# Two small MLPs of an attention branch, side by side on the columns of the array

## The chip, the cores and the metric

The kernel runs on one core of one Trainium2 chip. The metric is the device time of one execution in microseconds (us), a median over runs; less is better. A core has TensorE (PE; its weight loads are listed apart, as PEld), VectorE (DVE), ScalarE (ACT), GpSimd (POOL) and SyncE (SP), which here only issues DMAs.

## The reference

A two-layer decoder trunk on 512 tokens of width 1024. Each layer makes one input projection and hands parts of it to three token mixers: a gating MLP (its two inputs are za0 and za1 below), a retention, and a sparse attention. The last one has a compressed branch: keys and values of overlapping blocks of 32 tokens pass through a small MLP, one for the keys and one for the values.

```python
def compress(kv, pos_emb, w1, w2):
    Bn, S, G, d = kv.shape
    nc = (S - CMP_BLOCK) // CMP_STRIDE + 1          # 31 blocks
    idx = (jnp.arange(nc) * CMP_STRIDE)[:, None] + jnp.arange(CMP_BLOCK)[None, :]
    blocks = kv[:, idx] + pos_emb[None, None, :, None, :]
    flat = jnp.moveaxis(blocks, 3, 2).reshape(Bn, nc, G, CMP_BLOCK * d)
    return jax.nn.gelu(flat @ w1) @ w2              # (., 2048) @ (2048, 64), then @ (64, 64)
...
k_cmp = compress(k_c.reshape(Bn, S, G, d), pos_k, w1_k, w2_k)
v_cmp = compress(v_c.reshape(Bn, S, G, d), pos_v, w1_v, w2_v)
...
sc = jnp.einsum('bqgrd,bkgd->bgrqk', qb, k_cmp)
p_cmp = masked_softmax(sc, cmp_end[None, :] <= t[:, None])
o_cmp = jnp.einsum('bgrqk,bkgd->bqgrd', p_cmp.astype(dt), v_cmp)
```

## The kernel before

Each layer runs through the same stages on the core. Weights come from HBM through a ring of three raw buffers, issued on SP in a fixed order of jobs; ACT makes a rounded part of each (L125), DVE or, for some, POOL the difference (L127), and every large product is three PE passes on those parts (L535 to L537 for projections with tokens as rows, 128x256; L445 to L447 for those with features as rows). Where a projection is named a step, it is twelve such products: `tm_all` yields after each step, and four steps make half of za0 or za1.

The input projection first makes the raw keys and values of the compressed branch and the queries. `compress_in` (L497, DVE) adds the position embedding and writes F, one tile for the keys and one for the values: its free dimension is ordered head half, group, block, position, with eight positions innermost. `compress_load` fetches the weights: `w1` as sixteen blocks of 128x64 for each MLP, `w2` as a small tile.

Then za0 is projected (`tm_all`, ending in a GELU on ACT, L732). Then the compressed branch stands alone on PE: `compress_mm` multiplies the sixteen blocks of w1 with 62 columns of F, which lie eight values apart (L506), for the keys and then for the values, each in float32 into partitions 0 to 63 of its own PSUM tile. ACT applies GELU (L741 to hk, L744 to hid, a tile named t in the trace), PE multiplies with w2 (L747 for the keys, L749 twice for the values, named cw), ACT copies the keys out (L752, kc), DVE the values with a mask (L756, vcs), and `cmp_scores` multiplies kc with the queries on four 32-column strips of the array (L688), DVE adding a mask (L691, cs). Only then za1 is projected, its GELU giving Vv (L732).

Behind it come the projection of values and gates (L535 to L537 with 280 columns), the normalization of Vv on DVE (`norm64`, L464 to L475, with a power on POOL, L471), the softmax of the compressed scores (`cmp_softmax`, L699 to L715) between two key projections, and the transposes of its result (L724). In layer 1 `last_gains` also scales the residual xa by the gain and bias rows of the previous norm, two DVE passes a token tile (L1134, L1135 inside `gains`): tiles 0 and 1 behind the compressed branch, 2 and 3 behind za1.

The order on an engine is the program's, as a scheduler with a simulated timeline arranges it when the program is built; an engine then runs its list in order. PSUM has eight banks, given out in turn by `ps()`. For comparison, `retention` has products of the same shapes: L901 (128x64 weights, 64 columns, outputs alternating between partitions 0 and 64) and L892 (64 rows, alternating between the halves of the rows).

Of the kernel before, what the change touches and what calls it, by code (L numbers as in the profile page):

```python
# [22 lines left out]
L = 2  # L23
HD = 64
# [59 lines left out]
class Weights:  # L84
# [45 lines left out]
    def next(self, key, ahead=AHEAD, loads=3):  # L130
        i = self.i
        assert self.jobs[i][0] == key, (self.jobs[i][0], key)
        self.i += 1
        self.split(i)
        r = self.parts.pop(i)
        self.parts[i] = None
        raw = r.__class__ is not tuple
        for j in range(i + 1, i + 1 + ahead):
            if j < len(self.jobs) and self.jobs[j][1] != "raw":
                for j2 in range(i + 1, j):  # L140
                    self.load(j2)
# [7 lines left out]
def tile_trunk(ctx, tc, I, tab, out, layers=L):  # L149
    nc = tc.nc  # L150
    V, A, G, T = nc.vector, nc.scalar, nc.gpsimd, nc.tensor
# [3 lines left out]
    pool = ctx.enter_context(tc.tile_pool(name="sb", bufs=1))  # L155
    psum = ctx.enter_context(tc.tile_pool(name="ps", bufs=8, space=bass.MemoryType.PSUM))

    def ps():
        return psum.tile([P, 512], F32, tag="ps", name="ps")

    def t2(dt=F32):
        return pool.tile([P, 512], dt, tag="t2", name="t2", bufs=4)

    def m4(name):
        return pool.tile([P, 1024], F32, tag="m4", name=name, bufs=5)

    def big(name, dt=F32):
        return pool.tile([P, 13 * P], dt, tag="big", name=name, bufs=4)
# [13 lines left out]
    def load(dst, src):  # L182

        tc.keep_in_program_order(nc.sync.dma_start(dst, src))
# [47 lines left out]
    for l in range(layers):  # L232
# [16 lines left out]
        for n in range(32):  # L249
            if n % 8 in (0, 2):  # L250
                nm, c0 = (("rq", C_QB), ("rk", C_KB), ("rv", C_VB), ("rg", C_GB))[n // 8]
                h = n % 8 // 2
                job_cols((nm, l, h), l, [(c0, 256)], 4 * h, 4 * h + 4)
            if n in ADA_AT and aj:
                j = aj.pop(0)
# [25 lines left out]
    def tabv(name):  # L281
        a, b = TAB[name]
        return tb[:, a:b]
# [102 lines left out]
    def run(g):  # L386
        for _ in g:
            pass
# [89 lines left out]
    def compress_load(l):  # L478
        w1 = []
        for nm in ("c_w1_k", "c_w1_v"):  # L480
            w = big("w1")[:, :1024].rearrange("p (m e) -> p m e", m=16)
            load(w, I[nm][l].rearrange("(m p) e -> p m e", p=P))
            w1.append(w)
        w2 = pool.tile([P, 2, 256], F32, tag="al", name="cw2", bufs=1)[:64, :, :P]
        load(w2[:, 0, 0:64], I["c_w2_k"][l])
        load(w2[:, 0, 64:128], I["c_w2_k"][l])
        load(w2[:, 1, 0:64], I["c_w2_v"][l])
        return w1, w2

    def compress_in(pk, pos):  # L490
# [8 lines left out]
                                    op=OP.add)  # L499
        return F  # L500

    def compress_mm(F, w1):
        pc = ps()
        for m in range(16):
            h = m // 8
            T.matmul(pc[:64, :62], w1[:, m, :], F[:, h, :, h:h + 31, m % 8], start=(m == 0), stop=(m == 15))  # L506
        return pc

    for l in range(layers):
# [20 lines left out]
        def tm(wt, o, t, n, k0, k1, first, last):  # L530

            wh, wl = [w[:, :(k1 - k0) * n].rearrange("p (k n) -> p k n", n=n) for w in wt]
            for k in range(k0, k1):
                a, b = hx(hh, k, t, t + 1), hx(hl, k, t, t + 1)
                T.matmul(o, a, wh[:, k - k0, :], start=(first and k == 0), stop=False)  # L535
                T.matmul(o, a, wl[:, k - k0, :], start=False, stop=False)  # L536
                T.matmul(o, b, wh[:, k - k0, :], start=False, stop=(last and k == KD - 1))  # L537

        def tm_all(key, done):

            wts = []
            for tp in range(2):
                bank = ps()
                for h in range(2):
                    if not tp:
                        wts.append(ws.next(key + (h,)))
                    for s_ in range(2):
                        tm(wts[h], bank[:, s_ * 256:(s_ + 1) * 256], 2 * tp + s_, 256, 4 * h, 4 * h + 4,
                           s_ == 0, s_ == 1)
                        if h and s_:  # L550
                            done(tp, bank)
                        yield
# [13 lines left out]
        cmp_ps = []  # L566
        if l:
# [3 lines left out]
            for j in range(4):  # L571
                if j == 2:
                    last_h()
                banks.append(ps())
                wts.append(fm(keys[j], banks[j], 0))
            w1, w2 = compress_load(l)
            for j in range(6):
                if j < 4:
# [8 lines left out]
        else:  # L587
# [83 lines left out]
            for t in range(NT):  # L671
                G.tensor_scalar(X[t], X[t], ALPHA, None, op0=OP.mult)
            par = params(l)
            w1, w2 = compress_load(l)
            for j in range(2):
                cmp_ps.append(compress_in(banks[4 + j], par["pos"][j]))
# [7 lines left out]
        def cmp_scores(kc):  # L684
            for g in range(2):
                pc = ps()
                for r in range(4):
                    T.matmul(pc[32 * r:32 * r + 32, :], kc[:, g * 32:(g + 1) * 32], Q[g][:, r, :].bitcast(F32),  # L688
                             start=True, stop=True, tile_position=(0, 32 * r))
                CS.append(pool.tile([P, 512], F32, tag="yc", name="cs", bufs=2))  # L690
                V.tensor_tensor(CS[g], pc, mcmpb, op=OP.add)  # L691
# [36 lines left out]


        U, Vv = m4("U"), m4("Vv")  # L730
        for j, (nm, dst) in enumerate((("za0", U), ("za1", Vv))):
            run(tm_all((nm, l), lambda tp, pz, dst=dst: A.activation(  # L732
                dst[:, tp * 512:(tp + 1) * 512], pz, AF.Gelu_apprx_tanh)))
            if j == 0:

                hid = t2()[:64, :256].rearrange("p (g r n) -> p g r n", g=2, r=4)
                hk = pool.tile([64, 2, 32], F32, tag="hk", name="hk", bufs=1)
                G.memset(hid, 0.0)
                G.memset(hk, 0.0)
                pc = compress_mm(cmp_ps[0], w1[0])  # L740
                A.activation(hk[:, :, 0:31], pc[:64, :62].rearrange("p (g n) -> p g n", g=2), AF.Gelu_apprx_tanh)  # L741
                pc = compress_mm(cmp_ps[1], w1[1])
                for g in range(2):
                    A.activation(hid[:, g, :, 0:31],  # L744
                                 pc[:64, None, g * 31:(g + 1) * 31].to_broadcast([64, 4, 31]), AF.Gelu_apprx_tanh)
                pc = ps()
                T.matmul(pc[:, 0:64], w2[:, 0, :], hk.rearrange("p g n -> p (g n)"), start=True, stop=True)  # L747
                for g in range(2):
                    T.matmul(pc[:, 64 + 64 * g:128 + 64 * g], hid[:, g].rearrange("p r n -> p (r n)"),  # L749
                             w2[:, 1, 0:64], start=True, stop=True)  # L750
                kc = pool.tile([P, 64], F32, tag="kc", name="kc", bufs=1)
                A.copy(kc, pc[:, 0:64])  # L752
                vcs = pool.tile([P, 2, 2, HD], F32, tag="vcs", name="vcs", bufs=1)
                for g in range(2):
                    for s in range(2):
                        V.tensor_scalar(vcs[:, g, s, :], pc[:, 64 + 64 * g:128 + 64 * g],  # L756
                                        tabv("vm")[:, s:s + 1], None, op0=OP.mult)
                cmp_scores(kc)
            if l:
                for t in (2 * j, 2 * j + 1):  # L760
                    last_gains(t)


        VS = h4("vs", F32).rearrange("p b (t n) -> p b t n", t=NT)
# [1 line left out]
        pv = [ps() for _ in range(NT)]  # L766
# [46 lines left out]
        for b in range(2):  # L813
            pk = ps()
# [318 lines left out]
        def gains(t, lgr, lbr):  # L1133
            tc.keep_in_program_order(V.tensor_tensor(X[t], X[t], lgr, op=OP.mult))  # L1134
            tc.keep_in_program_order(V.tensor_tensor(X[t], X[t], lbr, op=OP.add))  # L1135
# [205 lines left out]
        if l + 1 < layers:  # L1341
# [3 lines left out]
            def last_gains(t, gains=gains, lgr=lgr, lbr=lbr):  # L1345
                gains(t, lgr, lbr)
# [28 lines left out]
```

## Time and profile before

| | us |
|---|---|
| median of 3 runs | 1427.34 (1426.94 to 1430.43) |
| the profiled execution | 1429.17 |
| span of its trace | 1427.2 |
| PE busy | 1368.5 (96%) |
| DVE busy | 889.6 (62%) |
| ACT busy | 549.4 (38%) |
| POOL busy | 213.8 (15%) |

The span is what the trace covers, from the first instruction to the last; 1.97 us of the profiled execution lie around it. Busy shares are averages over stages with different limits, and a PE that is busy all the time need not be at its peak: its passes overlap, and a pass's own length (293 ns, say) is longer than the step from one to the next. A step is therefore read from start to start.

### The profile page before, as it was taken

What the parts mean: (1) busy time and instruction counts of PE and PEld (TensorE: products, weight loads), DVE (VectorE), ACT (ScalarE), POOL (GpSimd) and SP (SyncE); (2) the same over time, 40 slices, a digit from 0 to 9 for tenths busy, and PEclk for the clock granted to TensorE, in tenths of its full rate; (3) what the DMA queues carried; (4) which work ended last, traced back from release to release, by engine and by line L of the source; (5) the groups of instructions that cost most, each with busy time, mean ns of one, the idle gap of its engine ahead of it and who ended that gap; (6) DMA issues with size and microseconds to landing.
All of it is one profiled execution on the core that took longest, in us unless ns stands there. A gap on an engine that the chain in (4) does not pass through costs nothing.

```text
span 1427.2 us, 19802 instructions
## 1 busy us (share of the span) xinstructions
PE 1368.5 (96%) x7794; PEld 1126.6 (79%) x7794; DVE 889.6 (62%) x1463; ACT 549.4 (38%) x999; POOL 213.8 (15%) x212
## 2 busy tenths in 40 slices
PE   6999999999899999999999989999999999999995
PEld 5898665679887788778879978877898888888884
DVE  6658436757899566843466577486566555764337
ACT  2425333552443343333324245456243334343220
POOL 0311220335211010000030023111510000000005
PEclk9999999999999999999999999999999999999998
DMA  9822454513988354422514131110323334332221
GB/s 280 220 71 89 148 163 155 170 47 91 315 283 265 99 170 124 142 92 89 149 29 118 43 103 45 45 45 30 89 62 94 97 95 127 96 125 90 102 75 59
DMA packets 188012, 168.91 MB, mean 118 GB/s; under 512 B 23526, under 2 KB 167758, under 8 KB 187920
## 3 DMA queue, kind: packets, MB, share of 16 engines
q1 hardware_dynamic: 180368, 141.18, 33.0%
q0 software_dynamic: 7552, 26.48, 5.5%
q8 instruction: 61, 1.00, 0.3%
q14 instruction: 31, 0.25, 0.1%
HBM read 163.44 MB, written 2.10 MB: 116 GB/s over the span
## 4 chain that ended last, share of the span: by engine, by line
PE 83%; DVE 7%; DMA 4%; issue 2%; POOL 1%; ACT 1%; SPq 1%; DVEq 0%; ACTq 0%; POOLq 0%
PE ps L446 19%; PE ps L447 19%; PE ps L445 19%; PE ps L535 4%; PE ps L536 4%; PE ps L537 4%; PE ps L998 3%; PE ps L324 2%; PE ps L990 2%; DMA a<-in_w_ada_dram 1%; PE ps L944 1%; PE ps L506 1%; PE ps L945 1%; DMA wraw<-in_w_up_dram 1%; PE ps L431 1%
## 5 line engine op out<-in xcount | busy, mean ns | idle before, releaser
L125 ACT CAST whi<-wraw 128x1024 fp32r<-128x1024 f32 (+4 forms) x188 | 186.6, 997 | 390.7 <-PE ps L446 208.2
L127 DVE TENSOR_TENSOR wlo<-wraw,whi 128x1024 fp32r<-128x1024 f32 (+3 forms) x162 | 187.4, 1159 | 184.0 <-ACT whi L125 183.6
L447 PE MATMUL ps<-h2h,wlo 128*128 128x512 f32 (+1 forms) x736 | 278.8, 379 | 0.0
L446 PE MATMUL ps<-h2l,whi 128*128 128x512 f32 (+1 forms) x736 | 277.6, 377 | 0.0
L445 PE MATMUL ps<-h2h,whi 128*128 128x512 f32 (+1 forms) x736 | 277.5, 378 | 0.0
L445 PEld LDWEIGHTS ps<-h2h,whi 128*128 128x128 f32 x736 | 138.9, 189 | 28.4 <-ACT whi L125 2.5
L446 PEld LDWEIGHTS ps<-h2l,whi 128*128 128x128 f32 x736 | 139.0, 189 | 27.1
L447 PEld LDWEIGHTS ps<-h2h,wlo 128*128 128x128 f32 x736 | 139.0, 189 | 26.1 <-issue 0.8
L535 PE MATMUL ps<-whi,hh 128*128 128x256 f32 (+1 forms) x448 | 131.7, 294 | 0.0
L536 PE MATMUL ps<-wlo,hh 128*128 128x256 f32 (+1 forms) x448 | 128.1, 286 | 0.0
L537 PE MATMUL ps<-whi,hl 128*128 128x256 f32 (+1 forms) x448 | 127.5, 285 | 0.0
L1141 POOL TENSOR_TENSOR xa<-xa,t 128x256 f32<-128x256 f32 (+1 forms) x30 | 35.8, 1200 | 527.2 <-DVE t L1140 527.2
L446 PE MATMUL ps<-wlo,pt 128*128 128x512 f32 x288 | 113.9, 396 | 0.0
L445 PE MATMUL ps<-whi,pt 128*128 128x512 f32 x288 | 113.9, 396 | 0.0
L447 PE MATMUL ps<-whi,pt 128*128 128x512 f32 x288 | 111.8, 396 | 0.0
L535 PEld LDWEIGHTS ps<-whi,hh 128*128 128x128 f32 x448 | 85.6, 191 | 15.2 <-issue 11.7
L536 PEld LDWEIGHTS ps<-wlo,hh 128*128 128x128 f32 x448 | 85.5, 191 | 3.6 <-issue 3.5
L537 PEld LDWEIGHTS ps<-whi,hl 128*128 128x128 f32 x448 | 85.4, 191 | 0.2 <-issue 0.2
L127 POOL TENSOR_TENSOR wlo<-wraw,whi 128x1024 fp32r<-128x1024 f32 x26 | 62.5, 2406 | 142.7 <-ACT whi L125 142.7
L187 DVE TENSOR_TENSOR pt<-g,pt 128x512 fp32r<-128x512 f32 x32 | 22.1, 691 | 81.5 <-PE ps L446 79.9
L991 ACT COPY pT<-ps 128x128 f32<-128x128 f32 (+3 forms) x128 | 50.2, 438 | 53.3 <-PE ps L990 52.9
L955 ACT ACTIVATE pt<-ps,sm 128x256 f32<-128x256 f32 (+2 forms) x96 | 55.8, 590 | 37.3 <-DVE sm L952 26.1
(272 smaller groups left out, 2682.4 us busy)
## 6 DMA issues: line engine op xcount, KB each, us to landing
wraw<-in_w_up_dram SPq DMA_DIRECT2D x88, 512.0 KB, 3.9
araw<-in_w_ada_dram POOLq DMA_DIRECT2D x48, 512.0 KB, 5.9
wraw<-in_w_down_dram SPq DMA_DIRECT2D x44, 512.0 KB, 3.5
wraw<-in_w_ada_dram SPq DMA_DIRECT2D x32, 512.0 KB, 3.4
wraw<-in_w_in_dram SPq DMA_DIRECT2D x30, 512.0 KB, 3.6
wraw<-in_w_out_dram SPq DMA_DIRECT2D x16, 512.0 KB, 4.1
a<-in_w_ada_dram SPq DMA_DIRECT2D x14, 512.0 KB, 7.2
wraw<-in_w_in_dram SPq DMA_DIRECT2D x8, 384.0 KB
```

Of the source, the lines that this page charges most:

```text
L125: self.nc.scalar.copy(f(hi), src)
L127: eng.tensor_tensor(f(lo), src, f(hi).bitcast(F32), op=OP.subtract)
L445: T.matmul(o, lh, rh, start=first, stop=False)
L446: T.matmul(o, lh, rl, start=False, stop=False)
L447: T.matmul(o, ll, rh, start=False, stop=last)
L535: T.matmul(o, a, wh[:, k - k0, :], start=(first and k == 0), stop=False)
L536: T.matmul(o, a, wl[:, k - k0, :], start=False, stop=False)
L537: T.matmul(o, b, wh[:, k - k0, :], start=False, stop=(last and k == KD - 1))
L955: A.activation(pp[e][:, :n], o[e], AF.Exp, bias=sm[:, 0, e:e + 1], accum_out=sm[:, 1, e:e + 1])
L991: A.copy(PT[e][:, i:i + 3 * i + 1:3, :], pb[:, :(i + 1) * P].rearrange("p (j q) -> p j q", q=P))
L998: T.matmul(po[64 * e:64 * e + 64, j * P:], VS[:, b, j, 64 * g:64 * g + 64], PT[e][:, 4 * j:4 * j + NT - j, :].rearrange("p a q -> p (a q)" ...
L1141: eng.tensor_tensor(X[t][:, c0:c0 + n], X[t][:, c0:c0 + n], tmp, op=OP.add)
```

## The change

`compress_mm` takes both MLPs at once: for each of the sixteen blocks it issues the product of the keys and then that of the values, into partitions 0 to 63 and 64 to 127 of one PSUM tile, with a tile position that names the column half of the array. hid and the value part of w2 move to partitions 64 to 127 for that; the products with w2 write two PSUM tiles in place of one. And the program is written in another order: after za0 come the gains of token tiles 0 and 1 (layer 1), then `compress_mm` and the GELUs, a step of za1, the products with w2 and their copies, another step of za1, the scores, and the rest of za1; the gains of tiles 2 and 3 stand at the end. The number of products is the same. Line numbers behind L500 shift: L506 becomes L508, L535 to L537 become L538 to L540, L688 and L691 become L691 and L694, L747 and L749 become L754 and L756, L756 becomes L763, L1134 and L1135 become L1143 and L1144.

```diff
-        w2 = pool.tile([P, 2, 256], F32, tag="al", name="cw2", bufs=1)[:64, :, :P]
-        load(w2[:, 0, 0:64], I["c_w2_k"][l])
-        load(w2[:, 0, 64:128], I["c_w2_k"][l])
-        load(w2[:, 1, 0:64], I["c_w2_v"][l])
+        w2 = pool.tile([P, 2, 256], F32, tag="al", name="cw2", bufs=1)[:, 0, :P]
+        load(w2[0:64, 0:64], I["c_w2_k"][l])
+        load(w2[0:64, 64:128], I["c_w2_k"][l])
+        load(w2[64:128, 0:64], I["c_w2_v"][l])
...
-    def compress_mm(F, w1):
+    def compress_mm(Fs, w1):
+
         pc = ps()
         for m in range(16):
             h = m // 8
-            T.matmul(pc[:64, :62], w1[:, m, :], F[:, h, :, h:h + 31, m % 8], start=(m == 0), stop=(m == 15))
+            for j in range(2):
+                T.matmul(pc[64 * j:64 * j + 64, :62], w1[j][:, m, :], Fs[j][:, h, :, h:h + 31, m % 8],
+                         start=(m == 0), stop=(m == 15), tile_position=(0, 64 * j))
         return pc
...
-        for j, (nm, dst) in enumerate((("za0", U), ("za1", Vv))):
-            run(tm_all((nm, l), lambda tp, pz, dst=dst: A.activation(
-                dst[:, tp * 512:(tp + 1) * 512], pz, AF.Gelu_apprx_tanh)))
-            if j == 0:
-
-                hid = t2()[:64, :256].rearrange("p (g r n) -> p g r n", g=2, r=4)
...
-                pc = compress_mm(cmp_ps[0], w1[0])
...
-                pc = compress_mm(cmp_ps[1], w1[1])
...
-                cmp_scores(kc)
-            if l:
-                for t in (2 * j, 2 * j + 1):
-                    last_gains(t)
+        run(tm_all(("za0", l), gelu_into(U)))
+        if l:
+            for t in range(2):
+                last_gains(t)
+
+        za1 = tm_all(("za1", l), gelu_into(Vv))
+        hid = t2()[64:128, :256].rearrange("p (g r n) -> p g r n", g=2, r=4)
...
+        pc = compress_mm(cmp_ps, w1)
...
+        next(za1)
+        pk, pv = ps(), ps()
+        T.matmul(pk[:, 0:64], w2[0:64, :], hk.rearrange("p g n -> p (g n)"), start=True, stop=True)
+        for g in range(2):
+            T.matmul(pv[:, 64 * g:64 * g + 64], hid[:, g].rearrange("p r n -> p (r n)"),
+                     w2[64:128, 0:64], start=True, stop=True)
...
+        next(za1)
+        cmp_scores(kc)
+        run(za1)
+        if l:
+            for t in range(2, NT):
+                last_gains(t)
```

On PE, layer 1, from the end of za0 on, this stood in a row before (a row ends in the shape of the product and, behind an x, how many follow each other; F_6630 holds the keys, F_6663 the values):

```order
L537 MATMUL ps_6863<-whi_6764,hl1_5575 128x256
L506 MATMUL ps_6917<-F_6630,w1_6598 64x62 x16
L506 MATMUL ps_6935<-F_6663,w1_6600 64x62 x16
L747 MATMUL ps_6954<-hk_6914,cw2_6602 128x64
L749 MATMUL ps_6954<-cw2_6602,t2_6913 128x64 x2
L688 MATMUL ps_6965<-q0_6445,kc_6958 32x512 x4
L688 MATMUL ps_6972<-q1_6446,kc_6958 32x512 x4
L535 MATMUL ps_6983<-whi_6801,hh0_5572 128x256
```

Now the same place reads as follows; the first "..." leaves out 28 products of L508 in the same alternation, the second 21 of za1, the third 17 of za1:

```order
L540 MATMUL ps_6863<-whi_6764,hl1_5575 128x256
L508 MATMUL ps_6921<-F_6630,w1_6598 64x62
L508 MATMUL ps_6921<-F_6663,w1_6600 64x62
L508 MATMUL ps_6921<-F_6630,w1_6598 64x62
L508 MATMUL ps_6921<-F_6663,w1_6600 64x62
...
L538 MATMUL ps_6957<-whi_6801,hh0_5572 128x256
...
L754 MATMUL ps_6977<-hk_6918,cw2_6602 128x64
L756 MATMUL ps_6978<-cw2_6602,t2_6917 128x64 x2
L539 MATMUL ps_6957<-wlo_6802,hh0_5572 128x256
...
L691 MATMUL ps_7001<-q0_6445,kc_6982 32x512 x4
L691 MATMUL ps_7008<-q1_6446,kc_6982 32x512 x4
```

Keys and values alternate product by product into one PSUM tile, 22 products of za1 stand between them and L754, and 18 between L756 and the scores. In layer 0 it is the same, but the first product of the keys is followed by five of za1 before the other 31 come.

On DVE, layer 1, this stood behind the last weight difference of za1 before (vcs and cs are the copies and masks of the compressed branch, xa the residual, L464 the start of the normalization of Vv):

```order
L127 TENSOR_TENSOR wlo<-wraw,whi 128x1024
L127 TENSOR_TENSOR wlo<-wraw,whi 128x840
L756 TENSOR_SCALAR vcs<-ps,tb 128x64 x4
L691 TENSOR_TENSOR cs<-ps,mcmpb 128x512 x2
L1134 TENSOR_TENSOR xa<-xa,lg 128x1024
L1135 TENSOR_TENSOR xa<-xa,lb 128x1024
L1134 TENSOR_TENSOR xa<-xa,lg 128x1024
L1135 TENSOR_TENSOR xa<-xa,lb 128x1024
L464 TENSOR_REDUCE nst<-Vv 128x8
```

And now:

```order
L127 TENSOR_TENSOR wlo<-wraw,whi 128x1024
L1143 TENSOR_TENSOR xa<-xa,lg 128x1024
L1144 TENSOR_TENSOR xa<-xa,lb 128x1024
L1143 TENSOR_TENSOR xa<-xa,lg 128x1024
L127 TENSOR_TENSOR wlo<-wraw,whi 128x840
L1144 TENSOR_TENSOR xa<-xa,lb 128x1024
L763 TENSOR_SCALAR vcs<-ps,tb 128x64 x4
L694 TENSOR_TENSOR cs<-ps,mcmpb 128x512 x2
L464 TENSOR_REDUCE nst<-Vv 128x8
```

The four passes over xa have moved ahead of vcs and cs. In layer 0 the order of DVE is unchanged there; some instructions of DVE, ACT and PE change places with a neighbour later, in layer 0's up projection and at the start of layer 1.

## Rows read from the trace of the kernel before

**Rows 1.** The page: the span, busy time of each engine in us (share of the span, instructions), and the shares of the chain that ended last, by engine.

```profile
span 1427.2 us, 19802 instructions
PE 1368.5 (96%) x7794; PEld 1126.6 (79%) x7794; DVE 889.6 (62%) x1463; ACT 549.4 (38%) x999; POOL 213.8 (15%) x212
...
PE 83%; DVE 7%; DMA 4%; issue 2%; POOL 1%; ACT 1%; SPq 1%; DVEq 0%; ACTq 0%; POOLq 0%
```

**Rows 2.** Sums over the stretch of the compressed branch, from its first product to the first product of za1, in layer 0 (81.38 to 92.07) and in layer 1 (791.95 to 802.65): its length, then busy us of each engine.

```profile
sum 10.69, PE 10.34 PEld 8.44 DVE 4.94 ACT 2.23 POOL 0.14; mean PE 3.44 PEld 2.81 DVE 1.65 ACT 0.74 POOL 0.05
...
sum 10.70, PE 10.35 PEld 8.44 DVE 2.56 ACT 2.23 POOL 0.00; mean PE 3.45 PEld 2.81 DVE 0.85 ACT 0.74 POOL 0.00
```

**Rows 3.** The timeline of the same place. Columns: start, length from the first start to the last end (us), engine, line, operation, out<-in, shape, count, and in brackets the engine's idle time before it and what ended it. Layer 0 down to 92.42, then the two ends of it in layer 1.

```profile
81.18 0.28 PE L537 MATMUL ps<-whi,hl 128*128 128x256 f32 x1
...
81.39 7.46 PE L506 MATMUL ps<-F,w 128*64 128x62 f32 x64
...
88.56 0.29 PE L506 MATMUL ps<-F,w 128*64 128x62 f32 x1
...
88.78 0.43 PE L747 MATMUL ps<-hk,cw 64*128 64x64 f32 x2
88.94 0.42 ACT L744 ACTIVATE t<-ps 64x124 f32<-64x124 f32 x2 [3.42 <-PE ps L506]
89.26 0.52 PEld L749 LDWEIGHTS ps<-cw,t 64*128 64x128 f32 x4 [0.19 <-ACT t L744]
...
89.96 0.21 ACT L752 COPY kc<-ps 128x64 f32<-128x64 f32 x1 [0.59 <-PE ps L749]
...
90.22 1.93 PE L688 MATMUL ps<-q,kc 128*32 128x512 f32 x16 [0.30 <-ACT kc L752]
...
92.08 0.38 PE L535 MATMUL ps<-whi,hh 128*128 128x256 f32 x1
92.30 0.28 PE L536 MATMUL ps<-wlo,hh 128*128 128x256 f32 x1
92.42 0.28 PE L537 MATMUL ps<-whi,hl 128*128 128x256 f32 x1
...
791.76 0.28 PE L537 MATMUL ps<-whi,hl 128*128 128x256 f32 x1
...
802.88 0.28 PE L536 MATMUL ps<-wlo,hh 128*128 128x256 f32 x1
```

**Rows 4.** The timeline of DVE around it: in layer 0, then in layer 1.

```profile
75.67 7.00 DVE L497 TENSOR_TENSOR F<-ps,pcol 64x256 f32<-64x256 f32 x16
82.70 2.17 DVE L127 TENSOR_TENSOR wlo<-wraw,whi 128x1024 fp32r<-128x1024 f32 x2
...
790.28 1.23 DVE L127 TENSOR_TENSOR wlo<-wraw,whi 128x1024 fp32r<-128x1024 f32 x1 [6.19 <-ACT whi L125]
793.48 1.03 DVE L127 TENSOR_TENSOR wlo<-wraw,whi 128x840 fp32r<-128x840 f32 x1 [1.98 <-ACT whi L125]
800.78 0.86 DVE L756 TENSOR_SCALAR vcs<-ps,tb 128x64 f32<-128x64 f32 x4 [6.26 <-ACT kc L752]
...
803.43 1.22 DVE L1134 TENSOR_TENSOR xa<-xa,lg 128x1024 f32<-128x1024 f32 x1
```

**Rows 5.** Behind it in layer 1: the timeline from the first half of Vv to the transposes of L724, DVE, ACT, POOL and PE, and last the sums of the stretch from 815 to 827 (length; busy us of PE, PEld, DVE, ACT and POOL, each with its instructions; granted clock; share of the DMA engines; GB/s).

```profile
808.71 0.60 ACT L732 ACTIVATE Vv<-ps 128x512 f32<-128x512 f32 x1 [7.96 <-PE ps L537]
...
809.34 0.69 DVE L464 TENSOR_REDUCE nst<-Vv 128x8 f32<-128x512 f32 x1 [1.04 <-ACT Vv L732]
...
826.76 1.04 PE L699 MATMUL ps<-tb,cs 128*128 128x128 f32 x8
...
828.74 2.41 POOL L127 TENSOR_TENSOR wlo<-wraw,whi 128x1024 fp32r<-128x1024 f32 x1 [2.38 <-ACT whi L125]
...
829.05 2.64 DVE L475 TENSOR_TENSOR Vv<-Vv,al 128x512 f32<-128x512 f32 x1
...
834.84 0.16 DVE L709 TENSOR_TENSOR csm<-csm,gates 128x16 f32<-128x16 f32 x1
...
835.18 2.77 POOL L127 TENSOR_TENSOR wlo<-wraw,whi 128x1024 fp32r<-128x1024 f32 x1 [4.03 <-ACT whi L125]
...
835.67 2.31 DVE L709 TENSOR_TENSOR csm<-csm,gates 128x16 f32<-128x16 f32 x1
...
838.46 1.09 PE L724 MATMUL ps<-tb,pt 128*128 128x128 f32 x4 [5.20 <-DVE pt L715]
...
815.00:827.00 12.00, 12.00 (x95) 12.00 (x94) 11.00 (x15) 5.44 (x11) 2.16 (x2) 1.00 0.50 149
```

**Rows 6.** Passes of other shapes: by line, the lengths of one in ns (min/median/max), first and last start, form; then the timeline of one group of L901 and one of L892.

```profile
L506 PE MATMUL ps<-F,w x128: 292/293/305, 81.4 to 799.1; 128*64 128x62 f32 x128
...
L901 PE MATMUL ps<-vb,rot x48: 222/222/271, 247.6 to 950.8; 128*64 128x64 f32 x48
...
L688 PE MATMUL ps<-q,kc x32: 592/592/617, 90.2 to 802.1; 128*32 128x512 f32 x32
...
247.56 0.31 PEld L901 LDWEIGHTS ps<-vb,rot 128*64 128x64 f32 x8
247.56 0.45 PE L901 MATMUL ps<-vb,rot 128*64 128x64 f32 x8
...
936.79 0.72 PE L892 MATMUL ps<-t 64*128 64x128 f32 x8
```

More of the change, by code (lines that the diff above doesn't have):

```diff
@@ L730, in tile_trunk @@
         U, Vv = m4("U"), m4("Vv")
-        for j, (nm, dst) in enumerate((("za0", U), ("za1", Vv))):
-            run(tm_all((nm, l), lambda tp, pz, dst=dst: A.activation(
-                dst[:, tp * 512:(tp + 1) * 512], pz, AF.Gelu_apprx_tanh)))
-            if j == 0:
-                hid = t2()[:64, :256].rearrange("p (g r n) -> p g r n", g=2, r=4)
-                hk = pool.tile([64, 2, 32], F32, tag="hk", name="hk", bufs=1)
-                G.memset(hid, 0.0)
-                G.memset(hk, 0.0)
-                pc = compress_mm(cmp_ps[0], w1[0])
-                A.activation(hk[:, :, 0:31], pc[:64, :62].rearrange("p (g n) -> p g n", g=2), AF.Gelu_apprx_tanh)
-                pc = compress_mm(cmp_ps[1], w1[1])
[L743 to L757, printed above, removed]
-                cmp_scores(kc)
-            if l:
-                for t in (2 * j, 2 * j + 1):
-                    last_gains(t)
@@ new lines, in gelu_into @@
+        def gelu_into(dst):
+            return lambda tp, pz: A.activation(dst[:, tp * 512:(tp + 1) * 512], pz, AF.Gelu_apprx_tanh)
+        run(tm_all(("za0", l), gelu_into(U)))
[4 more added lines that the diff above has]
+        hid = t2()[64:128, :256].rearrange("p (g r n) -> p g r n", g=2, r=4)
+        hk = pool.tile([64, 2, 32], F32, tag="hk", name="hk", bufs=1)
+        G.memset(hid, 0.0)
+        G.memset(hk, 0.0)
@@ new lines, in tile_trunk @@
+        pc = compress_mm(cmp_ps, w1)
+        A.activation(hk[:, :, 0:31], pc[:64, :62].rearrange("p (g n) -> p g n", g=2), AF.Gelu_apprx_tanh)
+        for g in range(2):
+            A.activation(hid[:, g, :, 0:31],
+                         pc[64:128, None, g * 31:(g + 1) * 31].to_broadcast([64, 4, 31]), AF.Gelu_apprx_tanh)
+        next(za1)
+        pk, pv = ps(), ps()
+        T.matmul(pk[:, 0:64], w2[0:64, :], hk.rearrange("p g n -> p (g n)"), start=True, stop=True)
+        for g in range(2):
+            T.matmul(pv[:, 64 * g:64 * g + 64], hid[:, g].rearrange("p r n -> p (r n)"),
+                     w2[64:128, 0:64], start=True, stop=True)
@@ new lines, in tile_trunk @@
+        kc = pool.tile([P, 64], F32, tag="kc", name="kc", bufs=1)
+        A.copy(kc, pk[:, 0:64])
+        vcs = pool.tile([P, 2, 2, HD], F32, tag="vcs", name="vcs", bufs=1)
+        for g in range(2):
+            for s in range(2):
+                V.tensor_scalar(vcs[:, g, s, :], pv[:, 64 * g:64 * g + 64],
+                                tabv("vm")[:, s:s + 1], None, op0=OP.mult)
+        next(za1)
[4 more added lines that the diff above has]
+                last_gains(t)
```

## The prediction

> **What bounds the kernel now.** I read the page's sums first: TensorE (PE) is busy for 1368.5 of 1427.2 us and 83% of the chain that ended last is PE, so a microsecond taken off PE is a microsecond off the kernel unless another engine holds PE up further on [rows 1]. Then a table by stage: the stretch that the change rewrites takes 10.69 us in layer 0 and 10.70 us in layer 1, and PE is busy for 10.34 and 10.35 of these [rows 2]. The PE timeline takes it apart. From the last step of the projection ahead of it (81.18) to the second step of the projection behind it (92.30) pass 11.12 us; two ordinary projection steps of 0.12 us would have stood there anyway, so the compressed branch costs PE 10.88 us. In layer 1 the same two rows stand at 791.76 and 802.88, which is 11.12 and 10.88 again [rows 3].
>
> In it are 64 passes of L506 (each float32 product shows as two passes), started from 81.39 to 88.56: 7.17 us for 63 steps, 0.114 us a step. Then come the small products with two short waits: L749's weights 0.19 us behind the GELU of L744, L688 0.30 us behind the copy of L752 [rows 3]. DVE idles 6.26 us in layer 1 before L756 and then does four passes over xa of 1.22 us each [rows 4]. At the end of the next stretch PE waits 5.20 us for DVE at L724, the largest wait of PE anywhere behind the change [rows 5].
>
> **Does the pairing double the rate?** L506 is a 128x64 product with 62 moving columns, one pass per 0.114 us. L901 is its nearest relative: also 128x64, float32, 64 columns, but with its outputs alternating between partitions 0 and 64, as the change will do. Its eight passes take 0.45 us, of which the last one's own length is 0.22: eight starts in 0.23 us, 0.058 a pair, and its eight loads are done in 0.31 us [rows 6]. Two column halves of the array thus run side by side there, with alternation costing nothing that shows. L688 says the same of four quarters: sixteen 592 ns passes in 1.93 us [rows 3, 6].
>
> But one L506 pass lasts 293 ns and one of L901 222 ns [rows 6], and its step is twice as long. What differs is the moving operand: L901 reads 64 neighbouring values, L506 reads every eighth value of F, 32 bytes apart. So L506's step is set by reading F, and the two halves would read two different F at once. No row shows two such strided streams together. The Trainium skill ("SBUF — State Buffer", section Specifications (TRN2)) has 16-byte lines that want at least two hits each for full bandwidth and a penalty at each crossing; with a step of 32 bytes every value is a crossing. The 0.114 us against 0.058 agree. Paid per stream, the penalty leaves the sum below as it is; paid by both halves at one place, it makes the first rival. The page does not say which.
>
> Bounds for a pair of passes: 0.058 us (L901, as if the stride cost nothing) and 0.228 us (two L506 steps, nothing beside anything). I take 0.114: the same instruction's own step, with both halves in parallel as in L901 and L688.
>
> **The sum, per layer.** Rates of a change of shape, all from rows 3: entering a tile shape takes 0.21 (81.18 to 81.39), leaving it 0.22 (88.56 to 88.78), and the first projection step afterwards 0.22 (92.08 to 92.30). Each inserted block replaces two projection steps (0.24). So a block costs 0.41 plus its inner steps.
> - Compress block: 16 weight blocks, two passes each, both halves at once: 31 steps of 0.114 = 3.53, with 0.41: 3.94.
> - L754 and L756, now on different halves of the array's rows and in different PSUM banks: L756's four passes set the length, L754 lies beside. L892 shows it: eight passes over two row halves in 0.72 less the last one's 0.27 = 0.45 [rows 6]. Block: 0.86.
> - Scores (L691, before L688): 90.22 to 92.08 includes the leaving, 1.86; with entry 0.21 and first step 0.22 less 0.24: 2.05.
> - Layer 0 only: the scheduler puts one compress product ahead and five projection products behind it before the rest; one more block, 0.52.
> Layer 0: 3.94 + 0.86 + 2.05 + 0.52 = 7.37, gain 3.51. Layer 1: 6.85, gain 4.03. Together 7.5 us.
>
> **What lies beside other work.** The GELUs of hk and hid (the latter 0.42 us on ACT [rows 3]) and their waits are hidden by 22 projection products in either layer, 2.6 us; the copy to kc (0.21) by 18 products, 2.2 us. If that cover failed, the old waits of at most about 0.5 us a layer come back. In layer 0 the value half of F is wanted sooner: before, after 32 passes, at 81.39 + 32 x 0.114 = 85.0; now after the first block of layer 0, near 82.4. DVE makes F in sixteen adds from 75.67, 7.00 / 16 = 0.44 us each [rows 4], the last eight for the value branch: the twelfth, its first half, ends near 80.9, the last at 82.67, and that half is wanted at the ninth weight block, near 84. No wait; if PE came to it at once, at most 0.3 us. The weights of the coming projection are subtracted on DVE from 82.70 to 84.87 [rows 4]; PE wants them after 86.
>
> In layer 1 DVE now does the gains of the first two token tiles ahead of vcs and cs. Four passes of 1.22 us plus one weight difference of 1.03 fit between 791.5 and 797.5, before the products that vcs waits for; queued behind are vcs and cs, and cs is read by PE only at L699, 826.76 before the change [rows 5]. I cost it at nothing. The loads on SP keep their order; one weight buffer is freed some 2 us later, for a load that is not wanted for 15 us.
>
> **Does the gain reach the end?** Behind the block DVE works 11.00 of 12 us [rows 5] and PE waits 5.20 us for it. That stretch starts with L464, which had waited 1.04 us for the projection's GELU, which had waited for PE [rows 5]; so DVE's work begins earlier by as much as PE does, and the wait should come along at its old length. Its size hangs on two places where DVE takes 2.64 and 2.31 us (the second for an operation that took 0.16 just before), both begun within 0.5 us after a POOL subtraction of 2.4 to 2.8 us [rows 5]. If the order of arrival flips there, 2 us per place come or go; I put nothing for it in the sum, and it widens the range both ways. Elsewhere the scheduler swaps some DVE instructions within the up projection; PE has no wait on them in that stage that I could shorten, so nothing.
>
> The profiled execution: 1427.2 span, 1429.2 with what lies around it; less 7.5 gives 1419.7 and 1421.7. The median of the runs is 1427.34, 1.8 below that execution; less 7.5: 1419.8.
>
> **Rivals.**
> 1. The two halves share the reading of F, or do not overlap at all: 63 steps of 0.114 again, 7.18 instead of 3.53 per layer. What remains is 7.54 - 2 x 3.65 = 0.24 us: 1427.1. For it: strided streams were never seen in pairs, and the change adds six changes of shape at about 0.2 to 0.4. Against: L901, L688. The Trainium skill ("TensorE: Matmul & The Clock Gate", section Part 3: Packing small matmuls — row/col tiling) says a weight load overlaps a running product only where the row groups differ; two column halves share theirs, so by that rule loads and products would queue and the time is that of this rival. The trace disagrees: L901's loads start among running products of the same rows. 0.13.
> 2. DVE in layer 1 is the bound, and PE only waits longer at L724: the 4.0 us of layer 1 turn into a wait of 9.2 us, gain 3.5: 1423.8. For it: 11.00 of 12 us. Against: L464's wait on PE. 0.08.
> 3. Partial overlap, about 0.15 us per pair: 2 x 31 x 0.036 = 2.2 us lost, 1422.0. 0.08.
> 4. Slower: alternating halves on every product drains the array, 0.1 us a time (the part of 0.21 over a step), and nothing overlaps. 62 alternations in the two layers cost 6.2 us against the 0.24 that is left: 1433.3. It decides from about 0.07 us per alternation and only without overlap. Against: L901 alternates and keeps 0.23 us for eight starts. 0.03.
> The forecast has 0.68.
>
> **How the numbers follow.** A measurement of this kernel can tell about 0.3%, 4.3 us, from no change. The forecast and rival 3 are faster, also with one flip at L724 against them: 0.76. Rivals 1 and 2 are within 4.3 us: 0.21. Rival 4 is slower: 0.03. The forecast's own range is 1418.3 to 1421.5; down to 1416.0 lie pairs at 0.058 us (2 x 31 x 0.056 = 3.5 us more) and one flip in favour; up to 1425.5 lie rivals 2 and 3 and a flip against. Rival 1 is left out.
>
> **What would show it.** Right: L508's 64 passes per layer in about 3.7 us with two starts per 0.114; no PE wait at L754, L756 or L691; the stage of L506 to the scores down from 10.7 us to about 7; L724's wait in layer 1 still near 5.2 us. Wrong: L508 over 7 us (rival 1), single starts 0.2 us apart (rival 4), a wait near 9 us at L724 (rival 2).

## The result, and the profile after

The changed kernel takes 1420.72 us (median of 4 runs, 1419.44 to 1422.19), the kernel before on the same chip 1428.86 (1426.94 to 1430.43): a ratio of 0.9937, 95% interval 0.9924 to 0.9951. That is 8.1 us less, and the time lies within the forecast's own range, 1418.3 to 1421.5. The first lines of the profile's page:

```profile
span 1419.0 us, 19802 instructions
...
PE 1360.1 (96%) x7794; PEld 1117.2 (79%) x7794; DVE 887.7 (63%) x1463; ACT 548.6 (39%) x999; POOL 216.1 (15%) x212
```

PE lost 8.4 us of busy time and the span 8.2; PE's share is as before. The PE timeline of layer 1 answers to [rows 3], from the last step of za0 to the end of the scores (left out are steps of za1, 0.12 us apart):

```profile
790.15 0.28 PE L540 MATMUL ps<-whi,hl 128*128 128x256 f32 x1
790.36 3.88 PE L508 MATMUL ps<-F,w 128*64 128x62 f32 x64
794.17 0.39 PE L538 MATMUL ps<-whi,hh 128*128 128x256 f32 x1
794.39 0.28 PE L539 MATMUL ps<-wlo,hh 128*128 128x256 f32 x1
...
796.78 0.28 PE L538 MATMUL ps<-whi,hh 128*128 128x256 f32 x1
796.99 0.32 PE L754 MATMUL ps<-hk,cw 64*128 64x64 f32 x1
797.00 0.32 PE L756 MATMUL ps<-cw,t 64*128 64x64 f32 x1
797.15 0.27 PE L754 MATMUL ps<-hk,cw 64*128 64x64 f32 x1
797.15 0.49 PE L756 MATMUL ps<-cw,t 64*128 64x64 f32 x3
797.58 0.39 PE L539 MATMUL ps<-wlo,hh 128*128 128x256 f32 x1
797.80 0.28 PE L540 MATMUL ps<-whi,hl 128*128 128x256 f32 x1
...
799.72 0.28 PE L538 MATMUL ps<-whi,hh 128*128 128x256 f32 x1
799.93 1.92 PE L691 MATMUL ps<-q,kc 128*32 128x512 f32 x16
801.78 0.39 PE L539 MATMUL ps<-wlo,hh 128*128 128x256 f32 x1
802.00 0.28 PE L540 MATMUL ps<-whi,hl 128*128 128x256 f32 x1
```

No row has a wait in brackets. The 64 passes of L508 take 3.88 us where L506 took 7.46, and a pass is no shorter than before:

```profile
L508 PE MATMUL ps<-F,w x128: 292/293/307, 81.6 to 793.9; 128*64 128x62 f32 x128
```

So twice as many passes are under way at a time. The starts of the first eight, one by one in the trace:

```
790.361 790.368 | 790.488 790.495 | 790.604 790.610 | 790.717 790.723
```

Two starts lie 6 or 7 ns apart (at most 17 in this layer), and the pairs follow each other every 0.11 us, which was the step of a single pass before. Layer 0 shows the single product that the scheduler put ahead:

```profile
81.39 0.28 PE L540 MATMUL ps<-whi,hl 128*128 128x256 f32 x1
81.60 0.42 PE L508 MATMUL ps<-F,w 128*64 128x62 f32 x2
81.95 0.38 PE L538 MATMUL ps<-whi,hh 128*128 128x256 f32 x1
82.17 0.28 PE L539 MATMUL ps<-wlo,hh 128*128 128x256 f32 x1
...
82.74 3.84 PE L508 MATMUL ps<-F,w 128*64 128x62 f32 x62
```

Behind the stretch, layer 1 answers to [rows 5]. The timelines of DVE, POOL and PE:

```profile
803.66 0.69 DVE L464 TENSOR_REDUCE nst<-Vv 128x8 f32<-128x512 f32 x1 [1.05 <-ACT Vv L735]
...
823.50 2.51 DVE L475 TENSOR_TENSOR Vv<-Vv,al 128x512 f32<-128x512 f32 x1
...
829.98 2.31 DVE L712 TENSOR_TENSOR csm<-csm,gates 128x16 f32<-128x16 f32 x1
...
823.07 2.40 POOL L127 TENSOR_TENSOR wlo<-wraw,whi 128x1024 fp32r<-128x1024 f32 x1 [2.25 <-ACT whi L125]
...
829.49 2.77 POOL L127 TENSOR_TENSOR wlo<-wraw,whi 128x1024 fp32r<-128x1024 f32 x1 [4.03 <-ACT whi L125]
...
832.77 1.08 PE L727 MATMUL ps<-tb,pt 128*128 128x128 f32 x4 [5.18 <-DVE pt L718]
```

DVE's chain starts behind the projection as before (a wait of 1.05 us against 1.04), its two long operations are still there, and PE waits 5.18 us at L727 where it waited 5.20 at L724. The chain moved as a whole.

### The profile page after: what moved, and what is told of

It is laid out like the page before. It is cut to its first block, busy times and chain, and to the rows that moved or that the text cites. A ratio compares the mean times of both kernels' runs of the same rounds, so it can differ in the third digit from the quotient of the medians.

```text
span 1419.0 us, 19802 instructions
## 1 busy us (share of the span) xinstructions
PE 1360.1 (96%) x7794; PEld 1117.2 (79%) x7794; DVE 887.7 (63%) x1463; ACT 548.6 (39%) x999; POOL 216.1 (15%) x212
## 4 chain that ended last, share of the span: by engine, by line
PE 85%; DVE 7%; issue 2%; DMA 2%; POOL 1%; SPq 1%; ACT 1%; DVEq 0%; POOLq 0%; ACTq 0%
PE ps L445 19%; PE ps L447 19%; PE ps L446 19%; PE ps L538 4%; PE ps L539 4%; PE ps L540 4%; PE ps L1007 3%; PE ps L324 2%; PE ps L999 2%; PE ps L953 1%; PE ps L954 1%; SPq L184 1%; DMA wraw<-in_w_up_dram 1%; POOL xa L1150 1%; PE ps L431 1%
## 5 line engine op out<-in xcount | busy, mean ns | idle before, releaser
L538 PE MATMUL ps<-whi,hh 128*128 128x256 f32 (+1 forms) x448 | 131.9, 294 | 0.0
L540 PE MATMUL ps<-whi,hl 128*128 128x256 f32 (+1 forms) x448 | 127.6, 285 | 0.0
L538 PEld LDWEIGHTS ps<-whi,hh 128*128 128x128 f32 x448 | 85.5, 191 | 14.8 <-issue 12.1
L540 PEld LDWEIGHTS ps<-whi,hl 128*128 128x128 f32 x448 | 85.4, 191 | 0.3 <-issue 0.3
L187 DVE TENSOR_TENSOR pt<-g,pt 128x512 fp32r<-128x512 f32 x32 | 22.1, 691 | 81.9 <-PE ps L446 76.9
```

## The experiments

Whole times differ by one or two us between executions. So one more figure is used below, the **stretch**: every kernel's trace has 7794 PE passes, and the passes 341 to 491 (layer 0) and 4321 to 4481 (layer 1) hold the same work in each: the end of za0, the compressed branch, steps of za1. From the start of the first to that of the last pass, in us:

| kernel | layer 0 | layer 1 | less than before, together | ratio of times, 95% interval |
|---|---|---|---|---|
| before | 18.55 | 19.75 | | |
| changed | 15.00 | 15.68 | 7.62 | 0.9937 (0.9924 to 0.9951) |
| e1 pairs, old order | 14.84 | 15.97 | 7.49 | 0.9940 (0.9922 to 0.9958) |
| e2 order alone | 18.61 | 19.81 | -0.12 | 0.9988 (0.9976 to 0.9999) |
| e3 changed, F unit stride | 13.14 | 13.89 | 11.27 | 0.9907 (0.9891 to 0.9924) |
| e5 before, F unit stride | 15.04 | 16.24 | 7.02 | 0.9939 (0.9919 to 0.9958) |
| e6 halves in turn | 17.64 | 18.84 | 1.82 | 0.9974 (0.9964 to 0.9983) |
| e11 e3 in the old order | 13.45 | 14.19 | 10.66 | 0.9912 (0.9896 to 0.9928) |
| e12 e3 again | 13.14 | 13.89 | 11.27 | 0.9904 (0.9890 to 0.9918) |

**e1: the pairs alone.**

```diff
-        if l:
-            for t in range(2):
-                last_gains(t)
         za1 = tm_all(("za1", l), gelu_into(Vv))
...
-        next(za1)
         pk, pv = ps(), ps()
...
-        next(za1)
         cmp_scores(kc)
+        if l:
+            for t in range(2):
+                last_gains(t)
         run(za1)
```

> The keys and values are paired as in the changed kernel, but the program order is that of the kernel before: GELUs, w2 products, scores, gains and only then za1. My theory (the pairs carry the gain, the order adds little): L508 still takes about 3.65 us per layer from first to last start (32 pairs, 0.114 us each), and the waits come back: about 0.4 us for the first product with w2 and as much for the second, since both GELUs now start together behind the last pair, and about 0.2 us for the scores. From the last step of za0 to the second step of za1 about 7.5 us per layer where the kernel before has 11.12, so 3.6 us a layer, 7.2 us in all: about 1420.5, ratio 0.995. Rival (the order carries half of it): a stretch of 9 us or more per layer, ratio 0.997 or above.

1420.5 us, ratio 0.9940: as expected. Of the three waits only the first came back, 0.31 us in layer 1 and 0.38 in layer 0; before the second w2 product and the scores PE is not idle. Layer 1, with the idle time in brackets (L749 and L751 are the w2 products here):

```profile
788.67 3.88 PE L508 MATMUL ps<-F,w 128*64 128x62 f32 x64
792.86 0.43 PE L749 MATMUL ps<-hk,cw 64*128 64x64 f32 x2 [0.31 <-ACT hk L744]
793.15 0.66 PE L751 MATMUL ps<-cw,t 64*128 64x64 f32 x4
793.74 1.92 PE L691 MATMUL ps<-q,kc 128*32 128x512 f32 x16
```

**e2: the order alone.** `compress_mm` and w2 as before, in the new program order:

```diff
-        pc = compress_mm(cmp_ps, w1)
+        pc = compress_mm(cmp_ps[0], w1[0])
+        pc2 = compress_mm(cmp_ps[1], w1[1])
...
-                         pc[64:128, None, g * 31:(g + 1) * 31].to_broadcast([64, 4, 31]), AF.Gelu_apprx_tanh)
+                         pc2[:64, None, g * 31:(g + 1) * 31].to_broadcast([64, 4, 31]), AF.Gelu_apprx_tanh)
```

> The products stay unpaired, keys first and then values, each into partitions 0 to 63 of a PSUM tile of its own; only the program order of the changed kernel is taken over. My theory: 64 passes of L506 at 0.114 us, 7.17 us per layer as before; no wait of TensorE before the w2 products and the scores, but two more changes of shape, so that a layer gains between 0 and 0.3 us: 1427, ratio 0.9985 to 1.0005. Rival (the order carries half): 3 to 4 us less, ratio 0.9975 or below.

Ratio 0.9988, inside the first range. L506 starts its 64 passes over 7.17 us again (the row's 7.46 less the last pass's 0.29):

```profile
794.13 7.46 PE L506 MATMUL ps<-F,w 128*64 128x62 f32 x64
```

The stretches are 0.06 us longer each: the waits saved are paid for in changes of shape. The rival falls with e1 and e2 together.

**e3: F with unit stride, in the changed kernel.**

```diff
-        F = big("F")[:, :1024].rearrange("p (h g n m) -> p h g n m", h=2, g=2, n=32)
+        F = big("F")[:, :1024].rearrange("p (h g m n) -> p h g m n", h=2, g=2, n=32)
...
-                    src = pk[64 * g:64 * g + 64, :].rearrange("p (n m a) -> p a n m", n=32, a=2)[:, a]
+                    src = pk[64 * g:64 * g + 64, :].rearrange("p (n m a) -> p a m n", n=32, a=2)[:, a]
...
-                                    pos[64 * a:64 * a + 64, None, 8 * h:8 * h + 8].to_broadcast([64, 32, 8]),
+                                    pos[64 * a:64 * a + 64, 8 * h:8 * h + 8, None].to_broadcast([64, 8, 32]),
...
-                T.matmul(pc[64 * j:64 * j + 64, :62], w1[j][:, m, :], Fs[j][:, h, :, h:h + 31, m % 8],
+                T.matmul(pc[64 * j:64 * j + 64, :62], w1[j][:, m, :], Fs[j][:, h, :, m % 8, h:h + 31],
```

> The changed kernel with F stored position first, block last, so that the 62 moving columns of a product are two runs of 31 neighbouring values in place of every eighth value; DVE then reads its input with a stride instead. My theory (the step of 0.114 us per pair is the reading of F): pairs start about every 0.058 us as in L901, L508 takes about 1.85 us per layer in place of 3.65, a pass lasts 222 ns in place of 293, and the whole gains 3.6 us on the changed kernel: about 1417, ratio to the kernel before 0.991. Rival (the step is set by something else, the sum over 16 products into one PSUM place or the weight loads): L508 stays at 3.65 us and the ratio at 0.994.

1416.92 us, as the first theory has it. The lengths of a pass (min/median/max):

```profile
L508 PE MATMUL ps<-F,w x128: 222/222/269, 81.8 to 789.5; 128*64 128x62 f32 x128
```

And layer 1's timeline:

```profile
787.61 2.08 PE L508 MATMUL ps<-F,w 128*64 128x62 f32 x64
```

First to last start 1.86 us, a pair every 0.058, and DVE writes F as fast as before (16 adds in 6.99 us). The prediction had called 0.114 us "set by reading F" on one comparison of two lines; here the stride alone changed.

**e4: the changed kernel again.**

> The changed kernel once more, unaltered, for a second profiled execution. In the first one 2.6 us of layer 0's gain of 3.6 us were lost again near 253 us, at a wait of L324 for a weight transfer (2.03 us, 0.93 before) and a lower granted clock behind it, while some 3.2 us came in addition in layer 1 behind 935 us and 0.9 us near 365 us. If these belong to the change, the same places show the same differences again, within 0.3 us. If they are chance of one execution, the wait at L324 near 253 us lies elsewhere (0.5 to 2 us), and the ratio stays at 0.994 all the same. The blocks of the compressed branch show 3.58 and 4.07 us less than before in both cases.

1421.03 us, ratio 0.9938 (0.9924 to 0.9952), and the stretches of the first execution again, 15.00 and 15.68 us. Two of the other differences were chance: the wait of L324 near 252 us was 1.27 us here, and passes 1401 to 1571 around it, which had the lower clock in the first execution (0.57 from 254 to 258 us, 1.00 here), took 25.13 us against 27.42; and 1.3 us of gain near 935 us were not there. Two came again: the 0.9 us near 365 us, and 2.2 us near 1029 us, which e9 looks into.

**e5: F with unit stride in the kernel before**, with e3's edits.

> The kernel before with F stored position first, block last, and nothing else: unpaired products, old order. My theory (a step of L506 is the reading of F, and halves run beside each other at any step): a pass lasts 222 ns, single passes start every 0.052 to 0.058 us as the pairs of e3 do, L506 takes about 3.5 us per layer in place of 7.17, and the time falls by 7 us: about 1422, ratio 0.995. The layout alone would then be worth as much as the pairing alone. Rival (the unpaired products have a floor of their own at 0.11 us, which the pairing took away, and the layout pays only behind it): L506 stays at 7.2 us, ratio 0.9995.

1420.57 us, L506 in 3.72 us per layer, one pass every 0.058 us:

```profile
788.82 3.94 PE L506 MATMUL ps<-F,w 128*64 128x62 f32 x64
```

The layout alone is worth 7.02 us of stretch, the pairs alone 7.49, both 11.27. Each halves the step, from 0.114 us a pass to 0.057 or 0.058, and together to 0.029; so the two do not add up.

**e6: the halves in turn.**

```diff
-        for m in range(16):
-            h = m // 8
-            for j in range(2):
+        for j in range(2):
+            for m in range(16):
+                h = m // 8
                 T.matmul(pc[64 * j:64 * j + 64, :62], w1[j][:, m, :], Fs[j][:, h, :, h:h + 31, m % 8],
```

> The changed kernel with its 32 products in another order: all sixteen of the keys into the lower half, then all sixteen of the values into the upper half, at the same tile positions. My theory (the gain is that two neighbouring products stand on different column halves): no pair is left, 64 passes start every 0.114 us, L508 takes 7.2 us per layer, and the time is that of e2 or of the kernel before, 1427 to 1429, ratio 0.998 to 1.0. Rival (the tile position itself makes a pass shorter, whoever its neighbour is): L508 in about 3.7 us, ratio 0.994.

Half a miss. Most pairs are gone, but L508 took 6.74 us from first to last start, not 7.2, and the ratio, 0.9974, lies below the range:

```profile
790.33 7.03 PE L508 MATMUL ps<-F,w 128*64 128x62 f32 x64
```

At the change from keys to values the trace has pairs all the same:

```
793.301 793.414 | 793.528 793.534 | 793.643 793.659 | 793.759 793.773 | 793.874 793.887 | 794.000 794.114
```

Four pairs, 0.43 us per layer. Where F is laid out like this, passes of one half start 0.11 us apart or more everywhere else, so the first values must have started beside the last four passes of the keys, ahead of passes that the program has first. No row names the half, so this is inferred; it speaks against the plain statement that an engine runs its list in order. The Trainium skill ("TensorE: Matmul & The Clock Gate", section Part 3: Packing small matmuls — row/col tiling) has weight loads pulled ahead out of a queue, but products in strict order; these starts speak against the second half of that.

The same place answers a rival that no run was made for: that any two products with other operands and another output would run side by side. In the kernel before and in e2, keys give way to values with another F, other weights and another PSUM tile, but on the same column half, and there the step stays at 0.113 to 0.114 us, without a pair. So it takes the other half.

e2's stretches are 0.97 us a layer longer than e6's. The four pairs make 0.43 of that; the rest lies beside a second difference, not tested by itself: w2's products stand in one block in e6 and in two in e2 (803.15 and 804.65 us there, in layer 1).

**e7 and e8: two distances between.** F with 2 or with 4 positions innermost (8 or 16 bytes from one moving value to the next), here for 2:

```diff
-        F = big("F")[:, :1024].rearrange("p (h g n m) -> p h g n m", h=2, g=2, n=32)
+        F = big("F")[:, :1024].rearrange("p (h g c n b) -> p h g c n b", h=2, g=2, n=32, b=2)
```

> The changed kernel with two positions innermost in F: the moving values lie 8 bytes apart in place of 32. Pairs as in the changed kernel. Read at L508 alone, since other engines' orders change with it. My theory (what costs is that each value needs a line of its own): with two values in 16 bytes, as the Trainium skill's page on SBUF has it, the pair's step is near 0.058 us and a pass lasts 222 ns. Rival (any stride costs the same): 0.114 us and 293 ns.

> The changed kernel with four positions innermost in F: the moving values lie 16 bytes apart. Pairs as in the changed kernel, read at L508 alone. My theory (a line of 16 bytes for each value): every value again needs a line of its own, so 0.114 us a pair and 293 ns a pass, as at 32 bytes. Rival (the cost grows with the distance): between 0.058 and 0.114 us, about 0.085.

Both as the theory has it, in one execution each (the line is L509 in these kernels; 8 bytes first, with the lengths of a pass and then layer 1's timeline):

```profile
L509 PE MATMUL ps<-F,w x128: 218/220/270, 81.8 to 787.0; 128*64 128x62 f32 x128
...
785.07 2.11 PE L509 MATMUL ps<-F,w 128*64 128x62 f32 x64
```

```profile
L509 PE MATMUL ps<-F,w x128: 290/292/307, 83.2 to 793.2; 128*64 128x62 f32 x128
...
789.66 3.82 PE L509 MATMUL ps<-F,w 128*64 128x62 f32 x64
```

From first to last start these are 1.89 and 3.53 us, as 1.86 at 4 bytes (e3) and 3.58 at 32. The cost is a step between 8 and 16 bytes, with nothing more at 32. The Trainium skill ("SBUF — State Buffer", section Specifications (TRN2)) has 16-byte lines that need two hits each for full bandwidth. The rows agree on where the step lies, 222 or 220 ns a pass at 4 and 8 bytes against 292 or 293 at 16 and 32; its size is from the rows alone.

**e9: the kernel before again.**

> The kernel before once more, unaltered, for a second profiled execution. From 1027 us to the first steps of the next stage, all kernels so far, the one with the order alone among them, are 2.1 to 2.3 us shorter than the first execution of the kernel before, and their wait of TensorE for L1151 there is 1.4 to 2.0 us against 2.20. If that belongs to that one execution, this run shows about 1.4 us there too, and the gains outside the two rewritten stretches are no part of the change. If it belongs to the kernel before, it is 2.2 again.

1428.84 us, and the wait near 1029 us is 1.45: the 2.2 us belonged to one execution, not to the kernel before. The sums of the same 4 us in the first execution and in this one (length; busy us of PE, PEld, DVE, ACT and POOL; granted clock; DMA share; GB/s):

```profile
1030.00:1034.00 4.00, 4.00 (x23) 4.00 (x24) 2.60 (x8) 2.59 (x6) 1.53 (x3) 0.58 0.00 0
...
1030.00:1034.00 4.00, 3.28 (x28) 3.28 (x29) 2.89 (x8) 1.95 (x5) 1.48 (x3) 1.00 0.04 11
```

So the 2.2 us are a wait that is 0.75 us longer and, for the rest, a granted clock of 0.58 behind it. The expectation was too broad: e3 and e7 lost their time there as well, and e11 later (waits of 1.98, 1.83 and 1.91 us, a granted clock of 0.59 to 0.63 over 4 us behind them), while e8 waited 1.85 us and kept the full clock. It comes and goes with executions. Layer 0's scores had a loss of their own instead. The PE timeline:

```profile
90.82 3.28 PE L688 MATMUL ps<-q,kc 128*32 128x512 f32 x16 [0.30 <-ACT kc L752]
```

And the sums around it:

```profile
90.00:94.00 4.00, 3.70 (x20) 0.93 (x19) 1.55 (x5) 0.21 (x1) 0.00 (x0) 0.57 0.00 0
```

The 16 passes that took 1.93 us in [rows 3] take 3.28 here, at a granted clock of 0.57: most of these 4 us at the lower level of 1.2 GHz, behind the waits of the compressed branch. Layer 0's stretch is 20.00 us long in place of 18.55.

**e10: the subtractions off POOL**, on top of e3.

```diff
-    on_pool = ("rq", "rk", "rv", "rg", "wo")
+    on_pool = ("rk", "rv", "rg", "wo")
```

> The kernel of e3, with the weight differences of the first retention projection (the two of POOL's L127 that lie beside the long DVE operations of layer 1, and one more, and as many in layer 0) on DVE in place of POOL. My theory (the 2.5 us of L475 and the 2.3 us of the second L712 come from POOL's subtraction running beside them): L475 takes 0.69 us and L712 0.16 there, DVE gains 3.9 us and takes on two subtractions of 1.2 us; the wait at L727 goes from 5.2 to about 3.7 us, the time to about 1415.5, ratio 0.990. Rival (these two are long for a reason of their own): they stay above 2 us, the wait grows to about 7.5 us, the time to 1419, ratio 0.993.

A miss in time, 1421.3 us (ratio 0.9943, 0.9920 to 0.9965, against e3's 0.9907), though the cause was right: both operations are short again. DVE and PE in layer 1:

```profile
823.61 0.68 DVE L475 TENSOR_TENSOR Vv<-Vv,al 128x512 f32<-128x512 f32 x1
824.21 1.22 DVE L127 TENSOR_TENSOR wlo<-wraw,whi 128x1024 fp32r<-128x1024 f32 x1
...
828.85 1.23 DVE L127 TENSOR_TENSOR wlo<-wraw,whi 128x1024 fp32r<-128x1024 f32 x1 [0.73 <-ACT whi L125]
...
831.27 1.38 DVE L187 TENSOR_TENSOR kl<-ps,kh 64x512 fp32r<-64x512 f32 x2
...
833.13 0.17 DVE L712 TENSOR_TENSOR csm<-csm,gates 128x16 f32<-128x16 f32 x1
...
833.36 1.09 PE L727 MATMUL ps<-tb,pt 128*128 128x128 f32 x4 [5.44 <-DVE csm L712]
```

The 4.2 us won (L475 2.76 to 0.68, L712 2.31 to 0.17) went to two subtractions of 1.22 and 1.23, a wait of 0.73 for ACT's part of the weights, and two operations of L187 (1.38) that now come ahead of the chain. So layer 1 gains nothing, and layer 0 loses. L727 waited 0.20 us there in e3; now it is:

```profile
121.72 0.63 PE L727 MATMUL ps<-tb,pt 128*128 128x128 f32 x4 [2.64 <-DVE pt L718]
```

The granted clock behind it is 0.66 from 122 to 127 us, where e3 has 1.00, and PE is 4.1 us later than in e3 when both are past. The Trainium skill ("SBUF — State Buffer", section Who interferes with whom) has a VectorE instruction with two SBUF inputs and a GpSimd one that reads SBUF exclude each other; L475 and L712 have two such inputs, and the rows agree.

**e11 and e12: the best order for the best layout.**

> Pairs and the F of e3, in the program order of the kernel before (e1 with the layout of e3). From the traces so far the rewritten stretch, counted over the same products of TensorE, is 3.55 and 4.07 us shorter in the two layers for the changed kernel, 3.71 and 3.78 for e1, 5.41 and 5.86 for e3. My theory (the order is worth next to nothing, since the scheduler's single product in layer 0 costs what the waits of layer 1 cost): 5.5 and 5.6 us here, L508 in 1.86 us in both layers, the same time as e3 within 1 us. Rival (with the pairs twice as quick the GELUs are less covered, and the order begins to pay): 0.5 us or more per layer behind e3.

> The kernel of e3 once more, for a narrower interval beside e11 on the same chip: ratio to the kernel before 0.9907 again (11.3 us of the two stretches are 0.9921, the rest was chance), between 0.990 and 0.9925; and against the changed kernel's 0.994 clearly below.

e11: 1417.02 us, 1.7 above e12's on the same chip, its stretches 0.31 and 0.30 us behind e3's: between theory and rival. Layer 1 gains 5.57 us on the kernel before, as the theory has it, layer 0 5.11 where it has 5.5. In layer 0 the theory overlooked that quick pairs catch up with DVE: no pass of L508 starts between 84.46 and 84.76, while the last add of F (0.43 us from 84.27 on) is made, and L508 takes 2.26 us in place of 1.86. e12: 1415.30 us (1414.53 to 1417.07), ratio 0.9904, as expected. Its interval lies below that of the changed kernel: this is the version that beats both.

## Why the prediction was right, point by point

- **The pairs.** "31 steps of 0.114 = 3.53": measured 3.58 (790.36 to 793.95, the last start). Taken from L901 and L688; e1, e2 and e6 show that neighbours on different halves are the cause, and e3 that the step itself was the reading of F, as the prediction argued from one comparison of two lines. Rivals 1, 3 and 4 fall with pairs every 0.11 us and partners at most 17 ns apart. The rule that rival 1 drew on, that loads overlap products only in other row groups (the Trainium skill, "TensorE: Matmul & The Clock Gate", section Part 3: Packing small matmuls — row/col tiling), does not hold here as it was used: loads of 133 to 159 ns on all 128 rows ran beside products on the same rows, a pair of them every 0.11 us.
- **The sum of a layer.** From the timeline above, each with the 0.24 us of two steps taken off: compress block 790.15 to 794.39, 4.00 (forecast 3.94); w2 796.78 to 797.80, 0.78 (0.86); scores 799.72 to 802.00, 2.04 (2.05); layer 0's single product 81.39 to 82.17, 0.54 (0.52). The stretches gain 3.55 and 4.07 us (3.51 and 4.03). The w2 block was 0.08 too dear: its inner part was taken from L892 at 0.45, and L756's four passes, with L754's beside them, start within 0.38 (797.00 to the last start at 797.38).
- **The cover.** PE has no wait at L754, L756 and L691. But e1 shows what the cover is worth: 7.49 of 7.62 us come without it. The order was thus next to no gain, as the 0.24 us that the first rival kept had said (e2: -0.12); with unit stride it is worth 0.61 us (e11).
- **DVE in layer 1.** Rival 2 would have had 9 us at L727; 5.18 came. The flip at the two long operations, left in the range, did not come; e10 shows what they hang on.
- **The total.** 7.5 forecast, 7.62 in the stretches, 8.1 and, in e4's set, 8.4 us in the medians. That the time itself came within 1 us of the forecast 1419.8 was in part luck: the kernel before took 1428.86 us this time and not 1427.34, and a gain 0.6 us larger made up for some of that. What lies beyond the stretches does not come from the pairs: all measured ratios of the table lie 0.0008 to 0.0017 below what their stretches give (1.1 to 2.4 us), e2's among them, which gained nothing there. The traces show where such differences sit. Outside the stretches the two profiled executions differ most where only one of them has the lower clock: near 1030 us (0.58 from 1030 to 1034 before, 1.00 from 1022 to 1026 after: 2.2 us), near 940 us (0.66 from 941 to 946 before, 1.00 from 934 to 939 after: 1.3 us) and, the other way, near 254 us (1.00 from 255 to 259 before, 0.57 from 254 to 258 after: 2.6 us lost). And where e1 to e4 were measured, on one chip, the granted clock is 0.9865 on average over 17 runs of the kernel before and 0.9872 to 0.9875 for the four kernels; that difference, taken of 1427 us, is 1.0 to 1.5 us by estimate. It is the size of the rest there, but the two agree less well for the later experiments, and why the kernel before should be granted less stays open.

## What to carry to other kernels

Read the step between starts, not the length of a pass, and ask what sets it: two products on different column halves hide a slow step behind each other, and a better layout of the moving operand halves it, each worth about 7 us here, and 11 together. A block of small products cost about 0.4 us here in changes of tile shape, so scattering it among large ones pays only where a longer wait goes. A wait that ends on an engine working almost without a pause moves when the engine's work moves (L727), and stays when one of its operations is made quicker at the price of another (e10).

## What was not expected of the hardware

- Float32 moving values 16 or 32 bytes apart make the step of these products 0.11 us, values 4 or 8 bytes apart 0.06; two halves with slow streams do not slow each other.
- In e6, four passes of one half began beside the other's although the program has them later, as far as the starts tell.
- In one execution of two of the kernel before, short waits of 0.2 and 0.3 us were followed by a granted clock of 0.57 for 4 us, at a cost of 1.35 us in the scores; the other had the same waits at full clock.
